# Residual rows loaded late, pair sums over one row, a weight fold moved forward and late loads issued by GpSimd, in a one-core step of a hybrid attention and Fourier network

## The chip, the cores and the metric

The kernel runs on one core of a Trainium2 chip. The metric is the device time of one launch in microseconds (us), taken as the median over several runs. A profile is one execution seen by the hardware profiler. Its engines are PE (TensorE, matmuls; PEld is its weight load), DVE (VectorE), ACT (ScalarE), POOL (GpSimd) and SP (SyncE, which only issues transfers here).

## The reference, cut to what matters

There are 1024 latent tokens and 256 context tokens of width 1024. One even layer and one odd layer run after each other, then a last RMS norm. The shape of the two layers:

```
hl = modulate(rms_norm(xl, norm_g[l]), shift, scale)       # both layers
# even layer: one projection, cut in parts
qa, ka, va, ga, qb, kb, vb, gb = split_even(h @ w_in)
oa = attention over all keys (q and k normed and rotated)  # mixer A, 8 q heads, 2 kv heads
ob = attention over a band of 3 x 128 keys + the context, with a sink logit   # mixer B
y  = concat(oa * silu(ga), ob * silu(gb)) @ w_out
# odd layer
u, gate = split(h @ w_in, 2)
y  = (real(fft2(u)) * silu(gate)) @ w_out
x  = x + gt * y                                            # both layers
```

The keys, the values and the rows after the last norm are the outputs.

## The kernel before, in words

The tokens are cut into ten rows of 128 (tiles 0 to 7 latent, 8 and 9 context). Every matmul is done three times, as hi by hi, hi by lo and lo by hi of operands that `split` (L265 to L283) cuts into a rounded part and a remainder: the hi copy is an ACTIVATE (L277), a DVE copy (L279) or a GpSimd copy, the lo part a subtraction (L283). Which engine takes which is set by letters in tables ("a", "d", "p", or an alternating string such as "pd").

SBUF is cut by hand into zones of equal buffers: 26 in zone u, 8 in w, 4 in p, 3 in pt, 2 in q, 9 short ones in h and 4 short ones in e. `take` hands out a buffer of a zone and `drop` gives it back; whoever takes a buffer next waits for its last reader, including a store to DRAM that reads it. Zone e holds what leaves the attention: the output pieces (`weigh`, L1051 to L1062, two buffers per unit, the second of them stored to `od` in DRAM by SP) and one row of reciprocal sums per tile (`totals`, L1018 to L1032, stored to `scd`).

The profiled execution falls into stages. From 0 to 100 us the conditioning vectors, norms and first projections are made; to about 440 us mixer A is attended; to about 690 us mixer B is attended, with the gate projections (`ga`, stored to `gd` in DRAM) between its units; to 866 us mixer B ends and the even output projection (`oz`) runs; from there come the odd layer's gates (`g1E`, `g1O`, `g1c`), its `u` projection, the Fourier transform and the last projection (`of`).

Attention is done in units: a tile t, a group g (2 and 3 are mixer B) and a pair pr of heads. A unit makes scores (`sC`, L928, against the context; `sB`, L1000, against the band), their maxima (L962, L1006), exponentials (ACT L969), transposes of the probabilities (`pt`, L1045), their hi and lo parts (ACT L277, DVE L1048) and the weighted values (`av`, L1051). Between the units stands filler: a queue of other matmul work, in the order of the string `ORDER`, of which a step runs when the unit's credit (2.9 per unit of mixer B, about microseconds) allows it. The last fillers are: the gates g2 and g3, interleaved by row group; the eight pairs of weight rows of `w_out0` (`wout_next`), loaded by SP into zone h and split into 16 buffers of zone u; the fold f3 of odd weights (`fold_load`, `fold_piece`, tiles `wa30` to `wa33`, L559); and ten steps of the even output projection, one for each row of 128 tokens, in the order of `PAIRS` (0, 4, 2, 6, 3, 7, 1, 5, 8, 9). Such a step may only run when the tiles that it reads are attended, and its load only when seven buffers of zones u and w are free. What is left when the attention ends is drained.

One step of that projection has two parts. `proj_in` (L1210 to L1233) loads a row of attention outputs (`od`, L1215), gates (`gd`, L1218), reciprocal sums (`scd`, L1220, two transfers) and the residual row (`xp`, L1232), multiplies the first three together (L1221, L1222, "pm") and splits the product. `out_proj` (L1235 to L1246) then makes two halves of 24 matmuls each, multiplies by the gate vector (L1243) and adds the residual row (L1244). `proj_step` stores the new row (L1343), takes its squared norm (L1344), and after each second row makes the sum and the difference of the two normed rows (L1356 to L1358), later sums of four rows (L1370 to L1377). These are transposed on PE (`eoE`, `eoO`, `eoC`, L1274) for the odd gates.

The transfers of `proj_in` are issued by GpSimd while the attention runs, and by SP once it has ended (L1211). The order in which each engine finds its instructions is set by a scheduler at build time, which follows the program, the buffers and a model of the times; each engine then works through its own list, and so does each issuing queue.

Of the kernel before, what the change touches and what calls it, by code (L numbers as in the profile page):

```python
# [17 lines left out]
P = 128  # L18
D = 1024
NT = 10  # L20
EPS = 1e-6
GROUPS = ((0, 4, 0), (4, 4, 0), (8, 2, 1))
ZONES = {"u": (26, 1032), "w": (8, 1032), "q": (2, 1024), "pt": (3, 1024), "p": (4, 1280), "h": (9, 512), "e": (4, 256)}
BIG = ("w", "q", "pt", "p", "u")
# [38 lines left out]
E_FQ, E_GD = "d", "d"  # L63
ORDER = "qa0 qa1 kb0 qb0 qb1 g0 g1 g2 g3"
FLATE = "f3"
AT_B = "s"
# [73 lines left out]
def hybrid_step(ctx: ExitStack, tc: tile.TileContext, I, O):  # L140
# [82 lines left out]
    pool.memset(SU, 0.0)  # L223
    rope = cp.tile([P, 8, 96], F32, name="rope")

# [358 lines left out]
    def small_loads(i):  # L584
        if i == 0:
            sp.dma_start(gT, I["gT"])
            sp.dma_start(bT, I["bT"])
            dve.tensor_scalar(bT1, bT[:, :, 8:16], 1.0, None, op0=ALU.add)
        elif i == 1:
            sp.dma_start(rope, I["rope"])  # L590
            sp.dma_start(gk, I["gk"].partition_broadcast(P))
            sp.dma_start(gq, I["gq"].partition_broadcast(P))
        else:
            sp.dma_start(sink, I["sink"].partition_broadcast(P))
            dve.tensor_scalar(nsink, sink, -1.0, None, op0=ALU.mult)
# [104 lines left out]
    def rope_pair(y, n, t, t1, t2):  # L700
        cb = rope[:, t : t + 2, 0:32].unsqueeze(2).to_broadcast([P, 2, 2 * n, 32])
        pick("rope", XE["rope"]).tensor_mul(  # L702
            t1.rearrange("p t h (b c) -> p t (h b) c", b=2), y.rearrange("p t h (b c) -> p t (h b) c", b=2), cb
        )
        for b in range(2):
            o, i = 32 * b, 32 - 32 * b
            sb = rope[:, t : t + 2, 32 + o : 64 + o].unsqueeze(2).to_broadcast([P, 2, n, 32])
            pick("rope", XE["rope"]).tensor_mul(t2[:, :, :, o : o + 32], y[:, :, :, i : i + 32], sb)
        pick("radd", XE["radd"]).tensor_add(t1, t1, t2)
# [389 lines left out]

    def out_weights(src, ks, tags, lc="pd"):  # L1100
        out = []
        for k in ks:
            hi, lo = take(tags, (P, D), F32R), take(tags, (P, D), F32R)
            for hf in range(2):
                raw = take("h", (P, 512))
                sl = slice(hf * 512, hf * 512 + 512)
                sp.dma_start(raw.a, src[k * P : (k + 1) * P, sl])
                split(hi[:, sl], lo[:, sl], raw.a, E_WO, lc)
                drop(raw)
# [25 lines left out]
    def wout_next(n):  # L1135
        for _ in range(n):
            fl_.add(0.0, lambda k=wk_left.popleft(): wout.extend(out_weights(I["w_out0"], (k,), UV)) or 0)

    for i, nm in enumerate(order[:-1]):
# [17 lines left out]
        if i < len(order) - 2:  # L1157
            fl_.add(0.0, releaser(nm))
# [51 lines left out]
    def proj_in(src, gate, r, resid):  # L1210
        ld = sp if gate is None or late[0] else pool  # L1211
        if gate is not None:
# [107 lines left out]
    def proj_step(i, j):  # L1320
# [36 lines left out]
        dve.scalar_tensor_tensor(out=xe.a, in0=xa.a, scalar=rs[:, 0:1], in1=xo_.a, op0=ALU.mult, op1=ALU.add)  # L1357
# [45 lines left out]

    def late_fold(nm):
        def fn():
            ws[nm] = fold_load(int(nm[1]))
            return 0
        return fn

    for n, nm in enumerate(FLATE.split()):  # L1410
        fl_.add(0.0, late_fold(nm))
        if n == 0:
            fl_.add(0.0, lambda: load_to(0), ready=can_run(0, 0))
        for k in range(4):
            fl_.add(FC, lambda k=k, nm=nm: fold_piece(int(nm[1]), k, ws[nm]))
    if not FLATE:
        fl_.add(0.0, lambda: load_to(0), ready=can_run(0, 0))
    for n, ij in enumerate(steps):
# [549 lines left out]
```

## Time and profile before

| What | Value |
|---|---|
| median of 3 runs | 1189.43 us |
| lowest and highest | 1188.47 and 1189.45 us |
| span of the profiled execution | 1196.9 us, 7.5 us above the median |
| PE busy | 1159.1 us, 97% |
| DVE busy | 834.5 us, 70% |
| ACT busy | 577.1 us, 48% |
| POOL busy | 286.0 us, 24% |

No other time of the profiled execution than its span is given, so the span stands for it. A busy time is the time in which an engine worked on at least one instruction. A row of the view by stretches gives the stretch, its length, then busy time (and instructions) of PE, PEld, DVE, ACT and POOL, then the granted TensorE clock (1.00 is full speed), the busy share of the transfer engines and GB/s. A row of the timeline gives start, length, engine, line, operation, tiles, shapes, count, and in brackets the idle time before it with what ended it. In a group of instructions the two numbers behind the bar are busy time in all and mean nanoseconds of one.

### The profile page before, as it was taken

What the parts mean: (1) busy time and instruction counts of PE and PEld (TensorE: products, weight loads), DVE (VectorE), ACT (ScalarE), POOL (GpSimd) and SP (SyncE); (2) the same over time, 40 slices, a digit from 0 to 9 for tenths busy, and PEclk for the clock granted to TensorE, in tenths of its full rate; (3) what the DMA queues carried; (4) which work ended last, traced back from release to release, by engine and by line L of the source; (5) the groups of instructions that cost most, each with busy time, mean ns of one, the idle gap of its engine ahead of it and who ended that gap; (6) DMA issues with size and microseconds to landing.
All of it is one profiled execution on the core that took longest, in us unless ns stands there. A gap on an engine that the chain in (4) does not pass through costs nothing.

```text
span 1196.9 us, 22002 instructions
## 1 busy us (share of the span) xinstructions
PE 1159.1 (97%) x8103; PEld 1037.9 (87%) x8103; DVE 834.5 (70%) x2006; ACT 577.1 (48%) x1159; POOL 286.0 (24%) x272
## 2 busy tenths in 40 slices
PE   8999999999999999999999989998999999999997
PEld 6788899999999998899888878886878888998886
DVE  2489778787777776678888867777755964367543
ACT  4442555555656655556676654532364225333211
POOL 2255644512222230011010035200212226200001
PEclk9999999999999999999999989998998999999999
DMA  9978512323532232444354477774214435364321
GB/s 327 365 257 272 160 59 69 89 77 113 148 89 78 76 95 84 100 120 116 83 148 105 131 223 203 232 224 160 85 45 136 147 115 167 109 186 150 141 105 54
DMA packets 130096, 168.81 MB, mean 141 GB/s; under 512 B 26298, under 2 KB 86454, under 8 KB 129988
## 3 DMA queue, kind: packets, MB, share of 16 engines
q1 hardware_dynamic: 127476, 158.74, 43.5%
q0 software_dynamic: 2368, 8.39, 2.3%
q8 instruction: 64, 1.05, 0.4%
q14 instruction: 44, 0.36, 0.1%
q10 hardware_dynamic: 144, 0.26, 0.1%
HBM read 123.19 MB, written 44.16 MB: 140 GB/s over the span
## 4 chain that ended last, share of the span: by engine, by line
PE 80%; DMA 9%; DVE 5%; ACT 2%; issue 2%; SPq 1%; POOL 1%; POOLq 0%; DVEq 0%; ACTq 0%
PE of L265 9%; PE q L265 8%; PE av L1051 8%; PE pt L1045 8%; PE ga L265 7%; PE sL L928 5%; PE u L265 5%; PE oz L265 4%; PE g1E L265 4%; PE g1O L265 4%; PE kv L265 3%; PE sC L928 2%; PE wa L559 2%; PE g1c L265 2%; DMA h<-i_w_out 2%
## 5 line engine op out<-in xcount | busy, mean ns | idle before, releaser
L277 ACT ACTIVATE pt<-pt 128x512 fp32r<-128x512 f32 (+1 forms) x265 | 146.8, 575 | 107.0 <-PE pt L1045 60.2
L1048 DVE TENSOR_TENSOR pt<-pt,pt 128x512 fp32r<-128x512 f32 (+1 forms) x264 | 170.8, 658 | 37.7 <-ACT pt L277 36.8
L1051 PE MATMUL av<-pt,u 128*128 128x256 f32 x1008 | 167.1, 289 | 0.7 <-ACT pt L277 0.7
L1045 PE MATMUL pt<-identr,p 128*128 128x128 f32 x1008 | 157.4, 273 | 1.1 <-ACT p L969 0.8
L265 PE MATMUL q<-w,u 128*128 128x256 f32 x960 | 143.9, 287 | 0.0
L1051 PEld LDWEIGHTS av<-pt,u 128*128 128x128 f32 x1008 | 138.9, 190 | 4.6 <-ACT pt L277 0.9
L265 PEld LDWEIGHTS q<-w,u 128*128 128x128 f32 x960 | 126.8, 188 | 4.9 <-issue 0.8
L1045 PEld LDWEIGHTS pt<-identr,p 128*128 128x128 f32 x1008 | 119.7, 141 | 8.0 <-ACT p L969 1.0
L969 ACT ACTIVATE p<-p,nm 128x1280 f32<-128x1280 f32 (+1 forms) x80 | 95.5, 1194 | 63.1 <-DVE p L962 62.8
L265 PE MATMUL ga<-u,w 128*128 128x512 f32 (+1 forms) x576 | 124.1, 360 | 0.8 <-DVE byp L1024 0.5
L265 PEld LDWEIGHTS ga<-u,w 128*128 128x128 f32 x576 | 93.6, 188 | 15.2 <-ACT pt L277 1.2
L283 POOL TENSOR_TENSOR w<-h,w 128x512 fp32r<-128x512 f32 x38 | 51.1, 1360 | 143.4 <-DVE w L279 115.0
L928 PE MATMUL sL<-u,q 128*128 128x512 f32 x256 | 82.4, 411 | 2.0 <-DMA q<-qd 2.0
L969 ACT ACTIVATE p<-p,NM 128x640 f32<-128x640 f32 (+2 forms) x80 | 59.2, 740 | 39.5 <-DVE p L962 39.4
L928 PE MATMUL sC<-u,q 128*128 128x256 f32 x320 | 61.8, 294 | 1.6 <-DMA q<-qd 1.0
L962 DVE TENSOR_SCALAR_CACHE_REDUCE p<-sL 128x512 f32<-128x512 f32 x64 | 43.9, 685 | 23.2 <-PE sL L928 14.2
L962 DVE TENSOR_SCALAR_CACHE_REDUCE p<-sL,nm 128x512 f32<-128x512 f32 x64 | 47.7, 745 | 13.7 <-PE sL L928 12.9
L265 PE MATMUL oz<-u,w 128*128 128x512 f32 x192 | 57.3, 403 | 0.0
L283 POOL TENSOR_TENSOR u<-h,u 128x512 fp32r<-128x512 f32 x16 | 20.6, 1293 | 138.0 <-ACT u L277 133.9
L928 PEld LDWEIGHTS sC<-u,q 128*128 128x128 f32 x320 | 48.8, 189 | 5.5 <-issue 1.1
L265 PE MATMUL oz<-u,u 128*128 128x512 f32 x160 | 48.7, 405 | 4.0 <-ACT u L277 2.5
L702 POOL TENSOR_TENSOR h<-h,rope 128x512 f32<-128x512 f32 (+1 forms) x18 | 21.9, 1214 | 126.4 <-ACT h L785 80.5
(728 smaller groups left out, 2569.8 us busy)
## 6 DMA issues: line engine op xcount, KB each, us to landing
q<-qd SPq DMA_DIRECT2D x80, 256.0 KB
h<-i_w_in SPq DMA_DIRECT2D x40, 256.0 KB
p<-i_ada_w SPq DMA_DIRECT2D x18, 512.0 KB
h<-i_w_out SPq DMA_DIRECT2D x32, 256.0 KB
pt<-i_ada_w SPq DMA_DIRECT2D x15, 512.0 KB
qd<-pt SPq DMA_DIRECT2D x20, 256.0 KB
q<-i_ada_w SPq DMA_DIRECT2D x9, 512.0 KB
qd<-q SPq DMA_DIRECT2D x18, 256.0 KB
```

The costliest lines, as they stand in the source:

```text
L265: pe.matmul(out, a, b, start=i == 0, stop=i == n - 1)
L277: act.activation(out, in_, AF.Copy)
L283: pick("lo" + lc, lc).tensor_sub(dst_l, src, dst_h)
L559: pe.matmul(acc[:, i * 256 : i * 256 + 256], wu[j][:, c0 : c0 + P], f[:, j, :], start=j == 0, stop=j == 1)
L702: pick("rope", XE["rope"]).tensor_mul(t1.rearrange("p t h (b c) -> p t (h b) c", b=2), y.rearrange("p t h (b c) -> p t (h b) c", b=2), cb)
L928: pe.matmul(ps, q_at(q, s, hc), keys, start=s == 0, stop=s == 1)
L962: dve.tensor_scalar(p[i][:, end[i] : end[i] + n], ps, sign, last[i], op0=ALU.mult, op1=ALU.min, accum_out=c)
L969: act.activation(p[i][:, 0 : end[i]], p[i][:, 0 : end[i]], AF.Exp, bias=last[i], scale=-1.0, accum_out=SU[:, t, hd + i, 0:1],)
L1045: pe.transpose(tp[:, jj * 256 + i * P : jj * 256 + i * P + P], p[i][:, off : off + P], ident)
L1048: dve.tensor_sub(pt[:, 1, 0:n], tp[:, 0:n], pt[:, 0, 0:n])
L1051: pe.matmul(acc, vv, pt[:, s, jj * 256 : jj * 256 + 256], start=c + jj + s == 0, stop=c + jj == nt - 1 and s == 1,)
```

## The change

It has five parts.

1. The table of cosines and sines (`rope`) is no longer a tile of its own, but three short buffers of zone e, which has seven buffers in place of four. They are loaded by three transfers, and dropped when the projection qb1 has ended; from then on zone e has seven buffers for the attention's outputs.
2. The fold f3 stands in the filler's order between the gates g1 and g2; before, it stood behind all gates and the splits of `w_out0`.
3. For `w_out0` both parts of `split` are GpSimd's: 16 hi copies that were ACT's, and all 16 lo subtractions, of which it had half.
4. The loads of a row of the even projection are issued by GpSimd always, the late ones too, and the residual row is taken and loaded only at the start of `out_proj`.
5. In the pair sums the second normed row is scaled in place, over the row that is being stored to `x1d`, and the difference goes over the first row: two buffers fewer are taken.

```diff
-ZONES = {... "h": (9, 512), "e": (4, 256)}
+ZONES = {... "h": (9, 512), "e": (7, 256)}
-ORDER = "qa0 qa1 kb0 qb0 qb1 g0 g1 g2 g3"
-FLATE = "f3"
+ORDER = "qa0 qa1 kb0 qb0 qb1 g0 g1 f3 g2 g3"
-    rope = cp.tile([P, 8, 96], F32, name="rope")
+    rope = [take("e", (P, 8, 32)) for _ in range(3)]
...
-            sp.dma_start(rope, I["rope"])
+            for i in range(3):
+                sp.dma_start(rope[i].a, I["rope"][:, i])
...
-    def out_weights(src, ks, tags, lc="pd"):
+    def out_weights(src, ks, tags, lc="pd", hc=E_WO):
...
-                split(hi[:, sl], lo[:, sl], raw.a, E_WO, lc)
+                split(hi[:, sl], lo[:, sl], raw.a, hc, lc)
...
+            if nm == "qb1":
+                drop(*rope)
...
-            fl_.add(0.0, lambda k=wk_left.popleft(): wout.extend(out_weights(I["w_out0"], (k,), UV)) or 0)
+            fl_.add(0.0, lambda k=wk_left.popleft(): wout.extend(out_weights(I["w_out0"], (k,), UV, "p", "p")) or 0)
...
+        elif nm[0] == "f":
+            work += [(FC, lambda k=k, nm=nm, j=j: fold_piece(j, k, ws[nm])) for k in range(4)]
...
-        ld = sp if gate is None or late[0] else pool
+        ld = sp if gate is None else pool
...
-        else:
-            for c in range(2):
+            return hi, lo, None
+        for c in range(2):
...
         hi, lo, xr = ins
+        if xr is None:
+            xr = take(OB[0], (P, D))
+            pool.dma_start(xr.a, I["xp"][r * P : (r + 1) * P, :])
...
-        xo_, xe = take(OB[0], (P, D)), take(OB[0], (P, D))
-        act.activation(xo_.a, xb.a, AF.Copy, scale=rs[:, 1:2])
+        xe, xo_ = take(OB[0], (P, D)), xa
+        act.activation(xb.a, xb.a, AF.Copy, scale=rs[:, 1:2])
...
-        drop(xa, xb)
+        drop(xb)
```

What this does to the engines' lists is seen at two places. The first is PE, some 27 us behind the last gate matmul of the profiled execution. Here `wa33` is the last piece of the fold f3, `sC`, `sB`, `pt` and `av` are attention (the digits give tile, group and pair), and `oz00` is the first output projection, of row 0. In the kernel before:

```order
L559 MATMUL wa33_9390<-h923_9286,w924_9288 128x256
L559 MATMUL wa33_9390<-h923_9286,w925_9289 128x256
L928 MATMUL sC9_20_9485<-u438_4475,q944_9420 128x256 x2
L928 MATMUL sC5_30_9692<-u687_7079,q953_9494 128x256 x2
L928 MATMUL sC9_21_9629<-u438_4475,q944_9420 128x256 x2
L1045 MATMUL pt6_310_9639<-identr_85,p948_9444 128x128 x4
L1051 MATMUL av8_21_9465<-pt949_9471,u438_4475 128x256 x4
L265 MATMUL oz00_9552<-u826_8504,w930_9305 128x512
L265 MATMUL oz00_9552<-u827_8505,w930_9305 128x512
```

In the changed kernel `oz00` begins here, three units of attention later:

```order
L1000 MATMUL sB1_310_9936<-u683_7067,q983_9711 128x384 x2
L1045 MATMUL pt5_304_9900<-identr_85,p982_9691 128x128 x2
L1051 MATMUL av9_20_9716<-pt984_9722,u441_4479 128x256 x4
L264 MATMUL oz00_9554<-u850_8685,w943_9398 128x512
L264 MATMUL oz00_9554<-u851_8686,w943_9398 128x512
L1000 MATMUL sB1_311_9941<-u683_7067,q983_9711 128x384 x2
L1045 MATMUL pt5_310_9949<-identr_85,p987_9735 128x128 x4
L928 MATMUL sC1_31_9929<-u685_7069,q983_9711 128x256 x2
L928 MATMUL sC8_30_10062<-u685_7069,q997_9870 128x256 x2
L264 MATMUL oz00_9554<-u850_8685,w944_9399 128x512
```

So `wa30` to `wa33` have gone from this stretch (they stand among the gates now), and between the last gate matmul `ga72` and `oz00` PE finds attention alone: 42 `pt`, 40 `av`, 24 `sC` and 16 `sB` matmuls, with no filler. Behind the last attention unit 237 `oz` matmuls are left, 193 before.

The second place is GpSimd's list at the loads of the first projection rows. `u908` and `u920` are lo parts of `w_out0`; `u927`, `u928` and `u929` are row 0's `od`, `gd` and `scd`, and `w960` belongs to row 4. In the kernel before:

```order
L283 TENSOR_TENSOR u908_9189<-h909_9190,u907_9188 128x512
L1215 DMA u927_9296<-od_72 128x1024
L1232 DMA w932_9309<-i_xp 128x1024
L283 TENSOR_TENSOR u920_9277<-h921_9278,u919_9276 128x512
L1220 DMA u929_9299<-scd_77 64x1024 x2
L1218 DMA u928_9298<-gd_73 128x1024
L1218 DMA w960_9539<-gd_73 128x1024
L1221 TENSOR_TENSOR u928_9298<-u928_9298,u929_9299 128x1024
L1222 TENSOR_TENSOR u927_9296<-u927_9296,u928_9298 128x1024
```

In the changed kernel row 0 has `u940`, `u941` and `u942`, row 4 has `w961`, `w962` and `w963`, and `u935`, `u936` are parts of `w_out0`:

```order
L278 CAST u935_9375<-h937_9377 128x512
L1222 DMA u940_9389<-od_72 128x1024
L1227 DMA w963_9542<-scd_77 64x1024 x2
L282 TENSOR_TENSOR u936_9376<-h937_9377,u935_9375 128x512
L1227 DMA u942_9392<-scd_77 64x1024
L1225 DMA u941_9391<-gd_73 128x1024
L1227 DMA u942_9392<-scd_77 64x1024
L1246 DMA w966_9552<-i_xp 128x1024
L1228 TENSOR_TENSOR w962_9541<-w962_9541,w963_9542 128x1024
L1222 DMA w961_9539<-od_72 128x1024
L1228 TENSOR_TENSOR u941_9391<-u941_9391,u942_9392 128x1024
L1229 TENSOR_TENSOR u940_9389<-u940_9389,u941_9391 128x1024
```

The product of row 0 now stands behind all 16 hi copies of `w_out0`, behind 8 lo subtractions more than before, and behind a product and a load of row 4.

More of the change, by code (lines that the diff above doesn't have):

```diff
@@ L22 @@
 GROUPS = ((0, 4, 0), (4, 4, 0), (8, 2, 1))
-ZONES = {"u": (26, 1032), "w": (8, 1032), "q": (2, 1024), "pt": (3, 1024), "p": (4, 1280), "h": (9, 512), "e": (4, 256)}
+ZONES = {"u": (26, 1032), "w": (8, 1032), "q": (2, 1024), "pt": (3, 1024), "p": (4, 1280), "h": (9, 512), "e": (7, 256)}
 BIG = ("w", "q", "pt", "p", "u")
@@ L700, in rope_pair @@
     def rope_pair(y, n, t, t1, t2):
-        cb = rope[:, t : t + 2, 0:32].unsqueeze(2).to_broadcast([P, 2, 2 * n, 32])
+        cb = rope[0][:, t : t + 2, :].unsqueeze(2).to_broadcast([P, 2, 2 * n, 32])
         pick("rope", XE["rope"]).tensor_mul(
@@ L706, in rope_pair @@
             o, i = 32 * b, 32 - 32 * b
-            sb = rope[:, t : t + 2, 32 + o : 64 + o].unsqueeze(2).to_broadcast([P, 2, n, 32])
+            sb = rope[1 + b][:, t : t + 2, :].unsqueeze(2).to_broadcast([P, 2, n, 32])
             pick("rope", XE["rope"]).tensor_mul(t2[:, :, :, o : o + 32], y[:, :, :, i : i + 32], sb)
@@ L1119, in fn @@
         def fn():
+            if nm[0] == "f":
+                ws[nm] = fold_load(int(nm[1]))
+                return 0
             ws[nm] = load_w(w0cols(base[nm[:-1]] + 256 * int(nm[-1])))
@@ L1156, in hybrid_step @@
             fl_.add(*w)
-        if i < len(order) - 2:
+        if i < len(order) - 2 and nm[0] != "f":
             fl_.add(0.0, releaser(nm))
@@ L1227, in proj_in @@
             drop(ol)
-        else:
-            for c in range(2):
-                split(hi[:, 4 * c : 4 * c + 4, :], lo[:, 4 * c : 4 * c + 4, :], src(c, r), "a", "d")
+            return hi, lo, None
+        for c in range(2):
+            split(hi[:, 4 * c : 4 * c + 4, :], lo[:, 4 * c : 4 * c + 4, :], src(c, r), "a", "d")
         xr = take(OB[0], (P, D))
@@ L1354, in proj_step @@
         kept.clear()
-        xo_, xe = take(OB[0], (P, D)), take(OB[0], (P, D))
-        act.activation(xo_.a, xb.a, AF.Copy, scale=rs[:, 1:2])
-        dve.scalar_tensor_tensor(out=xe.a, in0=xa.a, scalar=rs[:, 0:1], in1=xo_.a, op0=ALU.mult, op1=ALU.add)
-        dve.scalar_tensor_tensor(out=xo_.a, in0=xa.a, scalar=rs[:, 0:1], in1=xo_.a, op0=ALU.mult, op1=ALU.subtract)
-        drop(xa, xb)
+        xe, xo_ = take(OB[0], (P, D)), xa
+        act.activation(xb.a, xb.a, AF.Copy, scale=rs[:, 1:2])
+        dve.scalar_tensor_tensor(out=xe.a, in0=xa.a, scalar=rs[:, 0:1], in1=xb.a, op0=ALU.mult, op1=ALU.add)
+        dve.scalar_tensor_tensor(out=xo_.a, in0=xa.a, scalar=rs[:, 0:1], in1=xb.a, op0=ALU.mult, op1=ALU.subtract)
+        drop(xb)
         if i == 4:
@@ L1401, in load_to @@
         return 0
[L1404 to L1417, printed above, removed]
+    fl_.add(0.0, lambda: load_to(0), ready=can_run(0, 0))
     for n, ij in enumerate(steps):
@@ L1918 @@
     an = np.concatenate([ar, ac], axis=1)
-    rope = np.concatenate([np.cos(an), -np.sin(an), np.sin(an)], axis=1).reshape(8, 128, 96).transpose(1, 0, 2)
+    rope = np.concatenate([np.cos(an), -np.sin(an), np.sin(an)], axis=1).reshape(8, 128, 3, 32).transpose(1, 2, 0, 3)
     i = np.arange(128)
```

## The prediction

> **What bounds the kernel now.** I read the page first, then the busy time by stretches, then the timeline of PE where it falls short, then the waits and the chain for the causes.
>
> ```profile
> PE 1159.1 (97%) x8103; PEld 1037.9 (87%) x8103; DVE 834.5 (70%) x2006; ACT 577.1 (48%) x1159; POOL 286.0 (24%) x272
> 600.00:690.00 90.00, 87.55 (x592) 79.31 (x591) 76.68 (x236) 61.05 (x142) 9.84 (x8) 1.00 0.48 126
> 690.00:820.00 130.00, 117.28 (x636) 99.98 (x635) 93.16 (x212) 59.62 (x136) 33.03 (x32) 0.96 0.73 218
> 820.00:866.00 46.00, 46.00 (x197) 37.20 (x197) 34.06 (x46) 17.28 (x27) 9.10 (x8) 0.96 0.33 115
> ```
>
> PE is the bound, and no matmul is taken out. A change can only win what PE idles, or what it runs at less than full clock. Nearly all that the change touches lies between 600 and 866 us, where PE idles 90.00 - 87.55 = 2.45 us and 130.00 - 117.28 = 12.72 us. From 820 to 866 it is full.
>
> The second loss is the clock. Five microseconds at a time:
>
> ```profile
> 695.00:700.00 5.00, 1.73 (x4) 1.49 (x5) 2.31 (x7) 3.20 (x7) 2.54 (x4) 0.74 0.54 187
> 700.00:705.00 5.00, 5.00 (x22) 4.44 (x22) 2.65 (x8) 2.33 (x7) 0.83 (x2) 0.57 0.95 275
> 815.00:820.00 5.00, 1.77 (x6) 1.34 (x7) 3.47 (x4) 2.37 (x4) 0.31 (x1) 0.69 0.89 256
> 820.00:825.00 5.00, 5.00 (x15) 3.92 (x15) 4.00 (x6) 2.02 (x2) 0.00 (x0) 0.63 0.49 159
> 100.00:105.00 5.00, 2.66 (x80) 2.10 (x68) 4.97 (x12) 0.84 (x3) 2.15 (x3) 1.00 0.72 238
> ```
>
> Work at clock 0.57 takes 1/0.57 of its time, so of 5.00 us of busy time 2.15 are lost, and 1.73 x 0.26 = 0.45 before that: 2.6 us. At 815 to 825 it is 0.55 + 1.85 = 2.4 us. Both follow an idle stretch of 4 us or more. The last row is the other case: PE is idle for 47% of it, in 80 short matmuls' gaps, and the clock stays at 1.00.
>
> So the stage loses 2.45 + 12.72 + 2.6 + 2.4 = **20.2 us**. The four largest pieces of idle time on PE, and behind them what stood on the chain or kept ACT:
>
> ```profile
> 698.27 3.75 PE L559 MATMUL wa<-h,w 128*128 128x256 f32 x8 [4.51 <-ACT pt L277]
> 736.84 3.48 PE L265 MATMUL oz<-u,u 128*128 128x512 f32 x14 [1.59 <-DVE h L1243]
> 815.78 0.55 PE L1274 MATMUL eoE<-identr,p 128*128 128x128 f32 x3 [1.96 <-DVE p L1370]
> 818.78 1.22 PE L265 MATMUL oz<-u,u 128*128 128x512 f32 x2 [2.45 <-ACT u L277]
> 719.70 9.74 DMA od<-e
> 803.27 6.01 DMA u<-gd
> ACT u L277 <- DMA h<-i_w_out: 6.6, 1, 6.6
> ACT e L1030 <- DMA od<-e: 9.5, 1, 9.5
> ```
>
> The first gap names ACT's `pt`, but ACT itself had stood 6.6 us at the hi copy of a `w_out0` row that had not landed, with the attention's copies queued behind it. The other three belong to zone e: DVE or ACT wants a buffer that a store to `od` still reads, and what stands behind it on that engine (products, the squared norm, the hi copy `u`) comes late.
>
> **Part 1, zone e.** With seven buffers three more stores may be under way before `take` waits. A unit of attention holds one until its store has ended, and five units end in the 24 us of the stretch below, so three buffers cover some 15 us. The longest wait, 9.74 us, is shorter. I let these waits go: 1.59 + 1.96 + 2.45 us and the 2.4 us of clock. What is late next is in part 4. The three loads of the table lie at the start, and I take them at 0 (between -0.5 and +1 us).
>
> **Part 3, the splits of `w_out0`.** ACT is freed of 16 copies, and so of the wait: 4.51 us of idle time and 2.6 us of clock go. The cost falls on GpSimd.
>
> ```profile
> 681.19 2.99 PE L265 MATMUL ga<-u,w 128*128 128x256 f32 x24
> 687.39 2.70 PE L265 MATMUL ga<-u,w 128*128 128x256 f32 x21 [0.47 <-DVE byp L1024]
> L283 POOL TENSOR_TENSOR u<-h,u 128x512 fp32r<-128x512 f32 x8 | 10.3, 1293 | 111.9 <-ACT u L277 107.7 <-PE sB L1000 4.2
> L279 DVE CAST w<-h 128x512 fp32r<-128x512 f32 x36 | 16.7, 492 | 10.7 <-DMA h<-i_w_in 9.4 <-PE q L265 1.0 <-PE ga L265 0.3
> L1222 POOL TENSOR_TENSOR w<-w,w 128x1024 f32<-128x1024 f32 x3 | 7.8, 2613 | 0.3 <-DMA w<-od 0.2
> L1220 POOL DMA_DIRECT2D w<-scd x4 | 2.2, 547 | 0.8 <-issue 0.5 <-POOL w L1222 0.3
> w<-gd POOLq DMA_DIRECT2D x3, 512.0 KB, 7.6
> POOL w L1215 <- DMA od<-e: 6.2, 1, 6.2
> ```
>
> No GpSimd copy of 128x512 is in the trace. Its ends are DVE's copy, 0.49 us, and GpSimd's own subtraction, 1.29; I take 0.8, nearer to DVE's, which reads one operand too. In GpSimd's new list 8 copies, 8 subtractions and 10 transfers stand between the release by the gate `ga71` and the load of row 0's `od`: 8 x 0.8 + 8 x 1.29 + 10 x 0.55 = 22.2 us (19.7 to 26.1). From `ga71` to the last gate `ga72` lie four gates, 6.2 us apart as above: 24.8 us. So GpSimd is level with PE when `ga72` ends (call it T0) and can load row 0's `od`, for which it waits on `ga72`. Then come six more issues and a split, 0.55 x 6 + 1.29 = 4.6 us, the landing of `gd`, 7.6, and the two products of row 0, 2 x 2.6, which is some 17 us behind T0. A load of row 4 between them waits for a store to `od`, as now for 6.2 us, which `gd`'s landing hides.
>
> **Part 2, the fold.** The four `wa` pieces move from this stretch to one in which PE is full; they cost there what they save here. But they were filler. Between `ga72` and `oz00` PE now has attention alone:
>
> ```profile
> 723.80 1.43 PE L1051 MATMUL av<-pt,u 128*128 128x256 f32 x10
> 725.06 0.60 PE L1045 MATMUL pt<-identr,p 128*128 128x128 f32 x4
> 725.42 0.48 PE L928 MATMUL sC<-u,q 128*128 128x256 f32 x2
> 725.74 0.86 PE L1000 MATMUL sB<-u,q 128*128 128x384 f32 x4
> 726.44 5.71 PE L265 MATMUL oz<-u,w 128*128 128x512 f32 x24
> L1048 DVE TENSOR_TENSOR pt<-pt,pt 128x512 fp32r<-128x512 f32 x25 | 16.7, 677 | 0.2 <-ACT pt L277 0.2
> L962 DVE TENSOR_SCALAR_CACHE_REDUCE p<-sC,nsink 128x256 f32<-128x256 f32 x25 | 11.5, 469 | 0.8 <-PE sC L928 0.6
> L962 DVE TENSOR_SCALAR_CACHE_REDUCE p<-p,nm 128x384 f32<-128x384 f32 x12 | 7.0, 599 | 0.0
> L1006 DVE SCALAR_TENSOR_TENSOR p<-sB,maskf 128x384 f32<-128x384 f32 x12 | 6.4, 544 | 2.3 <-PE sB L1000 2.3
> L1062 DVE TENSOR_TENSOR e<-av,e 64x256 f32<-64x256 f32 x16 | 6.6, 410 | 5.3 <-DMA od<-e 3.2 <-ACT e L1060 2.1
> L283 DVE TENSOR_TENSOR u<-u,w 128x1024 fp32r<-128x1024 f32 x2 | 2.4, 1213 | 0.0
> L1021 DVE TENSOR_SCALAR tot<-tot 128x16 f32<-128x16 f32 x5 | 0.8, 161 | 0.0
> ```
>
> By the distances from start to start, 40 `av` at 0.126, 42 `pt` at 0.09, 24 `sC` at 0.16 and 16 `sB` at 0.175 make 5.0 + 3.8 + 3.8 + 2.8 = 15.4 us. DVE's list in the same piece of the program has 10 of L1048, 11 and 6 of L962, 8 of L1006, 5 of L1062, six small ones like L1021, and row 0's lo part, without which `oz00` can't go on: 6.8 + 5.2 + 3.6 + 4.4 + 2.1 + 1.0 + 1.2 = 24.3 us. GpSimd's product at 17 us, with its hi and lo part behind it (some 2.4, by DVE's 1.2 each), is there at 19.4 and hidden. So DVE sets the end, and PE idles **8.9 us** in short pieces, as at 100 to 105 us, where the clock stayed.
>
> One page's rule speaks against such pieces. The Trainium skill, TensorE: Matmul & The Clock Gate, section A second HAM failure mode: psum-queue depth-cycling, says that frequent micro-idles between groups of matmuls make the clock fall and rise again. The row at 100 to 105 us disagrees. It is the fourth rival below.
>
> **Part 4, the late loads.** Before, SP issued them; now they stand in GpSimd's list at 0.55 us each, behind products of 2.6 us and behind each other's waits. At the end DVE waits for the last loads (rows 1 and 5), and its lo parts behind them wait too. PE has 237 `oz` matmuls left there, but in their order the third matmuls of `oz50` and `oz11` need those lo parts. The price is between 0 (several rows of 24 matmuls, 5.7 us each, cover it) and 6.0, the longest wait for `gd` on the chain at the same place now. I take what DVE does after such a load, two products and a lo part: 3 x 1.22 = **3.7 us**. The late residual row costs nothing: it is needed only behind 24 matmuls of 5.7 us, about what a transfer of its size takes.
>
> Here another rule would give less. The Trainium skill, DMA: Bandwidth & Descriptors, section Issuing engines are not separate DMA queues, says that all transfers share the same 16 engines and that another issuer saves only the time of issuing, small beside the transfer. By that this part would cost nothing, and the sum would be 3.7 us lower. The 7.6 us of landing against 0.55 us of issue agree; what waits in GpSimd's list ahead of an issue is not in the rule.
>
> **Part 5, the pair sums.** ACT scales a row in place and so waits for its store to `x1d`; behind it on ACT stand the next row's norm and, in the drain, hi copies. PE is full there (46.00 of 46.00 us from 820 to 866), so between 0 and +1 I put 0.
>
> **The sum.** Lost after: 1.0 of the 2.45 us ahead of 690 (its waits, too, were mixed with the hi copies of `w_out0`), 8.9 in the filler-less stretch, 3.7 at the last rows, 1.0 of small waits as now: 14.6 us. Gain 20.2 - 14.6 = 5.6 us. From the span of 1196.9 that is 1191.3; the runs lie 7.5 us under the span, so their median comes to **1183.8 us**.
>
> **The rivals.**
>
> *More is kept.* A DVE instruction starts before the one ahead of it has ended:
>
> ```profile
> 810.58 0.69 DVE L1244 TENSOR_TENSOR pt<-pt,h 128x512 f32<-128x512 f32 x1
> 811.19 1.28 DVE L1357 SCALAR_TENSOR_TENSOR pt<-w,r11y,p 128x1024 f32<-128x1024 f32 x1
> ```
>
> That is 0.08 us; if all 47 of the stretch do so, they give back 3.7 us, and the last loads may be covered. Then 1.0 + 5.2 + 0 + 1.0 = 7.2 us are lost: gain 13.0, 1176.4 us. PE's longer backlog speaks for it, the one queue of GpSimd against it.
>
> *The stores weren't late for want of buffers.* If `od` stores and row loads are late because of the queues, seven buffers move the wait from zone e to the row products, and the 8.4 us at 735 and 812 to 825 stay beside 3.7 less: 14.6 + 8.4 - 3.7 = 19.3 lost, 1188.5 us, no difference. For it: the chain carries loads of rows too (6.01 us `u<-gd`), not `od` alone.
>
> *A store holds up GpSimd (slower).* Row 0's products stand behind row 4's load, which waits for tile 7's store to `od`. Stores of that kind held POOL for 6.2 us, and once for longer:
>
> ```profile
> POOL e L1512 <- DMA od<-e: 19.0, 1, 19.0
> ```
>
> If GpSimd stands 19.0 us from some 5 us behind T0, row 0's products are done at 29, its hi and lo part at 31.4, 7.1 us behind DVE's 24.3. The units are used up by then, so this is one piece, with 2.6 us of clock behind it, and part 4 goes to its 6.0: 12.0 us more, 1195.8 us. It decides from a wait of about 12 us on. A copy of 1.8 us or more would do the same, for which no row speaks.
>
> *The clock falls in the filler-less stretch (slower).* At half clock its 15.4 us of matmuls take 30.8, which is 6.5 above DVE's 24.3, and 2.6 us follow: 1192.9 us. It decides once PE's share of busy time there, 15.4 of 24.3 or 63%, is too low to hold the clock. Against it: at 100 to 105 us 53% held it.
>
> **How the numbers follow.** A measurement of this kernel can tell about 0.2%, 2.4 us, from no change: faster is below 1187.05, slower above 1191.8. The forecast gets 0.45, more kept 0.16, no difference 0.22, the store 0.08, the clock 0.09. Of the forecast's spread (part 4's 0 to 6.0, the table, part 5, 1183.8 -4.2 to +4.3) about a tenth falls within 0.2%; of the no difference a fifth is faster, and of the clock's case two fifths, milder, within. Faster: 0.40 + 0.16 + 0.04 = 0.60; within: 0.05 + 0.14 + 0.04 = 0.23; slower: 0.04 + 0.08 + 0.05 = 0.17. The range from 1177.0 to 1192.5 leaves out the lower half of the first rival, the store's case and the clock's upper half.
>
> **What would show it.** Right: ACT's wait for `i_w_out` and the waits for `od<-e` gone; PE below 70% busy at clock 1.00 for some 24 us behind `ga72`, released by DVE; an idle piece of 2 to 6 us at `oz50` or `oz11`. Wrong: a gap of over 4 us ahead of `oz00` ended by row 0's products on POOL (the store's case), clock rows of 0.5 to 0.7 in that stretch (the clock's), waits for `od<-e` as long as now (no difference), and a median above 1187.

## The result, and the profile after

The changed kernel took 1208.47 us in the median of 4 runs (1204.61 to 1211.85), the kernel before 1189.44 us: a ratio of **1.0146 (95% interval 1.0119 to 1.0174)**, 1.5% slower, where 1183.8 us had been forecast. One profiled execution is behind each page, and executions of one kernel differ by several microseconds: the changed kernel's took 1207.86 us at a span of 1206.1.

The page's first row, and the busy time by stretches:

```profile
PE 1157.3 (96%) x8103; PEld 1033.3 (86%) x8103; DVE 831.4 (69%) x1994; ACT 572.5 (47%) x1147; POOL 323.4 (27%) x326
600.00:690.00 90.00, 88.94 (x582) 80.52 (x581) 73.53 (x234) 55.60 (x130) 20.50 (x22) 1.00 0.42 108
690.00:820.00 130.00, 112.32 (x649) 96.32 (x650) 93.24 (x214) 57.26 (x133) 52.37 (x62) 0.95 0.67 191
820.00:866.00 46.00, 44.54 (x192) 34.94 (x191) 32.25 (x40) 14.18 (x19) 13.72 (x16) 1.00 0.53 175
```

The rows by stretches have the columns that were explained above. The same matmuls take the same busy time. PE idles 17.68 us from 690 to 820 us, 12.72 in the first profile of the kernel before. Most of that is one place, in rows of five microseconds and on PE's timeline:

```profile
710.00:715.00 5.00, 3.00 (x20) 2.11 (x19) 4.34 (x16) 4.31 (x15) 4.43 (x7) 1.00 0.99 237
715.00:720.00 5.00, 0.00 (x0) 0.00 (x0) 0.00 (x0) 0.00 (x0) 0.00 (x0) 0.57 1.09 250
720.00:725.00 5.00, 0.00 (x0) 0.00 (x0) 0.00 (x0) 0.00 (x0) 2.33 (x1) 0.50 1.05 225
725.00:730.00 5.00, 3.50 (x17) 3.53 (x18) 2.14 (x6) 0.51 (x2) 0.87 (x2) 0.57 0.85 186
```

```profile
713.05 0.66 PE L1045 MATMUL pt<-identr,p 128*128 128x128 f32 x4
726.50 0.76 PE L928 MATMUL sC<-u,q 128*128 128x256 f32 x2 [12.79 <-DMA q<-qd]
742.34 5.37 PE L264 MATMUL oz<-u,w 128*128 128x512 f32 x22 [0.63 <-DVE w L282]
```

For ten microseconds no engine computes, but for one product on GpSimd, and the transfer engines are full (the last column but one, 1.09 and 1.05). PE waits 12.79 us for a q load, in the stretch without filler behind the last gate. What the transfer engines carry is seen on the issuers. SP issues the second half of that load at 712.68, GpSimd two rows' loads around it:

```profile
709.93 0.59 SPq L933 DMA_DIRECT2D q<-qd  x1
712.68 0.63 SPq L933 DMA_DIRECT2D q<-qd  x1
```

```profile
690.55 0.61 POOL L278 CAST u<-h 128x512 fp32r<-128x512 f32 x1 [8.50 <-DMA h<-i_w_out]
707.46 0.61 POOL L278 CAST u<-h 128x512 fp32r<-128x512 f32 x1 [6.31 <-DMA h<-i_w_out]
708.01 0.58 POOL L1222 DMA_DIRECT2D u<-od  x1
710.47 1.04 POOL L1227 DMA_DIRECT2D w<-scd  x2 [1.88 <-DMA scd<-e]
713.30 0.55 POOL L1225 DMA_DIRECT2D u<-gd  x1
714.36 0.57 POOL L1246 DMA_DIRECT2D w<-i_xp  x1
720.06 2.33 POOL L1228 TENSOR_TENSOR w<-w,w 128x1024 f32<-128x1024 f32 x1 [5.14 <-DMA w<-scd]
729.11 0.61 POOL L1222 DMA_DIRECT2D w<-od  x1 [6.72 <-DMA od<-e]
732.22 2.39 POOL L1229 TENSOR_TENSOR u<-u,u 128x1024 f32<-128x1024 f32 x1
```

256 KB issued at 712.68 are used at 726.50, 13.8 us later. Between 708 and 715 GpSimd let go 2.5 MB (one `od`, two pairs of `scd`, one `gd`, one residual row). The last number of each row below is the time from issue to landing. The `od` row, the first of them, needed 4.0 us; the other 2 MB needed 8.6 to 14.0 us:

```profile
u<-od POOLq DMA_DIRECT2D x1, 512.0 KB, 4.0
w<-scd POOLq DMA_DIRECT2D x2, 256.0 KB, 8.6
u<-scd POOLq DMA_DIRECT2D x2, 256.0 KB, 10.0
u<-gd POOLq DMA_DIRECT2D x1, 512.0 KB, 10.6
w<-i_xp POOLq DMA_DIRECT2D x1, 512.0 KB, 14.0
```

Of the forecast's signs, the first came: on DVE and ACT no wait for `od<-e` is left, and ACT's wait for `i_w_out` is gone from this stage and stands on GpSimd instead, where a copy takes 616 ns (the rows below). The others did not: behind `ga72` the longest piece ends with a transfer and not with DVE, the clock falls, and at the last projection rows PE's longest idle piece is 1.11 us.

```profile
POOL u L278 <- DMA h<-i_w_out: 16.6, 4, 8.5
L278 POOL CAST u<-h 128x512 fp32r<-128x512 f32 x16 | 9.8, 616 | 87.8 <-DMA h<-i_w_out 46.4 <-PE ga L264 41.4
```

### The profile page after: what moved, and what is told of

Read it like the earlier page. It is cut to its first block, busy times and chain, and to the rows that moved or that the text cites. A ratio compares the mean times of both kernels' runs of the same rounds, so it can differ in the third digit from the quotient of the medians.

```text
span 1206.1 us, 22001 instructions
## 1 busy us (share of the span) xinstructions
PE 1157.3 (96%) x8103; PEld 1033.3 (86%) x8103; DVE 831.4 (69%) x1994; ACT 572.5 (47%) x1147; POOL 323.4 (27%) x326
## 3 DMA queue, kind: packets, MB, share of 16 engines
q8 instruction: 64, 1.05, 0.4%
## 5 line engine op out<-in xcount | busy, mean ns | idle before, releaser
L264 PEld LDWEIGHTS ga<-u,w 128*128 128x128 f32 x576 | 93.8, 188 | 17.2 <-ACT e L1060 2.5
L264 PE MATMUL oz<-u,w 128*128 128x512 f32 x304 | 83.0, 397 | 1.4 <-DVE w L282 1.0
L264 PEld LDWEIGHTS oz<-u,w 128*128 128x128 f32 x304 | 56.2, 188 | 14.8 <-DVE w L282 1.7
L962 DVE TENSOR_SCALAR_CACHE_REDUCE p<-sL,nm 128x512 f32<-128x512 f32 x64 | 47.7, 746 | 13.9 <-PE sL L928 13.2
L702 POOL TENSOR_TENSOR h<-h,e 128x512 f32<-128x512 f32 (+1 forms) x18 | 21.9, 1219 | 125.8 <-ACT h L785 79.9
L264 PE MATMUL of<-u,u 128*128 128x512 f32 (+1 forms) x174 | 55.4, 386 | 0.0
```

What stands on the lines that cost most here:

```text
L264: pe.matmul(out, a, b, start=i == 0, stop=i == n - 1)
L702: pick("rope", XE["rope"]).tensor_mul(t1.rearrange("p t h (b c) -> p t (h b) c", b=2), y.rearrange("p t h (b c) -> p t (h b) c", b=2), cb)
L962: dve.tensor_scalar(p[i][:, end[i] : end[i] + n], ps, sign, last[i], op0=ALU.mult, op1=ALU.min, accum_out=c)
```

## The experiments

All ratios are against the kernel before, run beside them on the same chip, with their 95% intervals; two versions are called different only where their intervals lie apart. "Lost" below is PE's idle time and busy x (1 - clock), added over rows of two microseconds of the profiled execution. That is one execution; the last column says how far its run lay above (+) or below the median of its kernel. For the first profile of the kernel before, whose run has no time of its own, this is an estimate: its span of 1196.9 us and the 1.8 us by which the changed kernel's span lies below its run. The names: zone e (part 1), fold (part 2), splits (part 3), late loads and residual row (the two halves of part 4), pair sums (part 5).

| Kernel | ratio (interval) | lost 690 to 760 | lost 760 to 870 | run against median |
|---|---|---|---|---|
| before, first profile | | 10.1 | 8.2 | about +9 |
| before, second profile | 0.9996 (0.9969 to 1.0023) | 2.6 | 6.7 | -1.2 |
| changed | 1.0146 (1.0119 to 1.0174) | 17.6 | 2.9 | -0.6 |
| changed, splits undone | 1.0243 (1.0208 to 1.0278) | 7.9 | 21.9 | -0.7 |
| changed, fold undone | 1.0142 (1.0100 to 1.0184) | 8.1 | 14.5 | -1.4 |
| changed, late loads undone | 1.0137 (1.0099 to 1.0174) | 21.2 | 5.4 | +1.0 |
| changed, residual row undone | 1.0100 (1.0054 to 1.0147) | 15.2 | 5.8 | -1.0 |
| changed, pair sums undone | 1.0086 (1.0055 to 1.0118) | 15.1 | 0.0 | -3.7 |
| changed, zone e undone | 1.0158 (1.0112 to 1.0203) | 17.2 | 11.5 | +1.3 |
| before + zone e | 1.0060 (1.0031 to 1.0090) | 6.1 | 12.3 | +3.0 |
| before + fold | 1.0079 (1.0053 to 1.0104) | 13.2 | 4.3 | +3.0 |
| before + splits | 1.0007 (0.9991 to 1.0024) | 9.0 | 8.5 | +4.1 |
| before + residual row | 1.0065 (1.0042 to 1.0089) | 3.5 | 12.7 | -2.5 |
| before + pair sums | 1.0052 (1.0034 to 1.0070) | 7.0 | 12.1 | +6.4 |
| changed, fold and pair sums undone | 1.0059 (1.0040 to 1.0078) | 8.4 | 9.8 | -0.1 |
| changed, less to load | 1.0186 (1.0152 to 1.0221) | 14.8 | 12.3 | -2.4 |
| changed, q earlier | 1.0115 (1.0086 to 1.0145) | 17.5 | 6.0 | -0.4 |
| changed, q earlier, pair sums undone | 1.0125 (1.0101 to 1.0150) | 14.5 | 9.3 | +0.6 |

**The kernel before, again.** No edit.

> The kernel before, unchanged, for a second profile of it. Its profiled execution of before had a span of 1196.9 us, 7.5 us above the median; the changed kernel's span is 1.8 us below its own run. If spans always lie 1.8 us below the run, the execution shown in the first profile was itself some 9 us slower than usual, and this one should have a span of about 1187.6 us. Then one of the two large pieces that the prediction counted, 4.51 + 2.6 us at 698 or 1.96 + 2.45 + 2.4 us at 816, should be missing or much shorter. If the 7.5 us are the profiler's, the span is again near 1197.

The span was 1189.6 us. The 6.6 us that ACT had stood for `i_w_out` are 1.4 here and the piece at 698 is gone; the piece at 816 is there, 1.17 + 2.45 us:

```profile
690.00:820.00 130.00, 122.32 (x676) 104.69 (x675) 100.90 (x221) 64.08 (x143) 33.36 (x32) 0.99 0.75 225
707.65 0.48 PE L928 MATMUL sC<-u,q 128*128 128x256 f32 x2 [1.64 <-DMA q<-qd]
809.06 0.55 PE L1274 MATMUL eoE<-identr,p 128*128 128x128 f32 x3 [1.17 <-DVE p L1370]
812.06 0.73 PE L265 MATMUL oz<-u,u 128*128 128x512 f32 x2 [2.45 <-ACT u L277]
ACT u L277 <- DMA h<-i_w_out: 1.4, 1, 1.4
```

So the execution on which the prediction rested had a stall that this one does not have, and the runs side with this one. PE idles 7.68 us in this stretch, not 12.72, at a clock of 0.99. This is the profile with which the others are compared.

**The splits undone.**

```diff
-            ... out_weights(I["w_out0"], (k,), UV, "p", "p")) or 0)
+            ... out_weights(I["w_out0"], (k,), UV)) or 0)
```

> The changed kernel with the splits of w_out0 as before (hi copies on ACT, lo parts on GpSimd and DVE in turn). Theory of the bundle: GpSimd's list with 16 more copies runs late, then lets go 2.5 MB of row loads within 7 us, and the attention's q load, issued among them, needs 13.8 us: PE idles 12.8 us. Without the copies the loads go earlier and apart: gap below 6 us, 1195 to 1200 us. Theory of the filler: the gap is there because the fold is gone from it, whoever splits w_out0: 1204 to 1210 us.

Neither theory's time came. The loss behind the last gate fell from 17.6 to 7.9 us as the first theory wanted (the wait for q is 3.33 us), and the kernel got slower by 1%: 21.9 us are lost at the end of the attention, the largest piece this one:

```profile
828.13 1.22 PE L264 MATMUL oz<-u,w 128*128 128x512 f32 x2 [5.33 <-DVE e L1062]
```

**The fold undone.** The fold stands behind the gates again (`FLATE = "f3"`, `ORDER` without f3).

> The changed kernel with the fold f3 late again, behind the gates. Theory of the filler: its 7.6 us of matmuls lie under the wait for q and the gap falls by about that: 1198 to 1201 us. Theory of the bundle: the row loads stay bunched; f3's own matmuls stand in PE's list ahead of the wait or behind it, and only what stands ahead helps: 1202 to 1209 us.

The filler does lie under the wait: 8.1 us lost in place of 17.6. But what is saved there is lost again where the last rows are projected:

```profile
710.72 1.19 PE L929 MATMUL sC<-u,q 128*128 128x256 f32 x4 [3.69 <-DMA q<-qd]
813.23 1.22 PE L1052 MATMUL av<-pt,u 128*128 128x256 f32 x4 [4.09 <-DVE e L1063]
819.95 7.13 PE L265 MATMUL oz<-u,w 128*128 128x512 f32 x24 [5.50 <-DVE e L1063]
```

**The late loads undone.** `ld = sp if gate is None or late[0] else pool`.

> The changed kernel with the late loads, those after the attention, issued by SP again. The bundle lies before the attention's end and stays: 1204 to 1209 us by both theories. If the late loads on GpSimd were the cause (the prediction's part 4, 3.7 us), 1203 to 1205 us, and PE's short idle pieces between 785 and 830 us go.

No difference can be told from the changed kernel, and the wait for q is there again, 12.88 us. The late loads on GpSimd are not the cause.

**The residual row undone** (taken and loaded in `proj_in`).

> The changed kernel with the residual row taken and loaded in proj_in again, one buffer more for each waiting row. Theory of the bundle, in its later form: what the versions with +1.4% share is that fewer buffers and GpSimd's list let two rows' loads go together with the q loads. With the residual row back in proj_in, the condition of seven free buffers is met later and the rows come apart: 1193 to 1200 us, and the wait for q under 6 us. Theory of the filler (the fold's place alone): no difference to the changed kernel, 1205 to 1211 us.

1.0100, below the changed kernel's 1.0146, but the intervals overlap, and the time lies between the two theories'. The wait for q is 6.55 us.

**The pair sums undone** (rows of their own).

> The changed kernel with the pair sums over rows of their own, as before. The in-place scaling waits for the store to x1d (5.6 us once on ACT in the profile of the changed kernel); the pair sums lie behind the wait for q. Theory of the bundle: 1204 to 1209 us, the wait for q stays at 12 us or so. If the in-place pair sums are the cause, PE's idle pieces at 785 to 830 and 880 to 890 us go, some 4 us: 1201 to 1205 us.

About 0.6% better. The wait for q stays, 10.49 us. From 760 to 870 us 0.0 us are lost in place of 2.9, but this execution is 3.7 us faster than the kernel's median, so the usual run may lose more.

**Zone e undone** (four buffers, the table a tile of its own).

> The changed kernel with the table of cosines as a tile of its own and four buffers in zone e. By the prediction's part 1 the waits for od stores come back: 6 to 8 us more, 1212 to 1217 us. By the loss of 3 us in the first 100 us of the changed kernel (11.36 idle against 8.39), which would be the three loads' doing: 3 us less at the start. If zone e was never the bound: 1203 to 1208 us.

No difference to the changed kernel (1.0158 and 1.0146, with intervals that overlap). The wait for q is not there; in its place DVE waits for zone e, and PE for DVE:

```profile
725.83 2.47 PE L1050 MATMUL av<-pt,u 128*128 128x256 f32 x10 [9.66 <-DVE e L1061]
```

Seven buffers take this wait away, and the q load is late instead, in the same crowd of transfers.

**Zone e alone.**

```diff
-"e": (4, 256)}
+"e": (7, 256)}
-    rope = cp.tile([P, 8, 96], F32, name="rope")
+    rope = [take("e", (P, 8, 32)) for _ in range(3)]
...
```

> The kernel before with only the table moved and seven buffers in zone e. By the prediction's part 1 the waits for od stores go, which in the second profile of before are 1.17 + 2.45 us at 809 to 814 us: 3 to 5 us faster than before. If those waits only move, within 2 us of before. If the three loads cost 3 us at the start, 0 to 3 us slower.

Slower by 0.6%, which none of the three expectations had. Waits for `od<-e` are all but gone on ACT (0.3 us), and at the longest piece DVE now stands for a row of reciprocal sums that hasn't landed, with the attention's `e` and the copy `ssp` behind it:

```profile
821.53 1.22 PE L1052 MATMUL av<-pt,u 128*128 128x256 f32 x4 [6.14 <-DVE ssp L1354]
819.92 1.23 DVE L1224 TENSOR_TENSOR q<-q,u 128x1024 f32<-128x1024 f32 x1 [2.88 <-DMA u<-scd]
```

**Less to load.** For rows 0 and 4, GpSimd writes constants over the buffers of the reciprocal sums and the residual row, which aren't loaded; the two rows' results are not those of the reference.

```diff
+            if r in (0, 4):
+                pool.memset(rl.a, 1.0)
+            else:
...
+            if r in (0, 4):
+                pool.memset(xr.a, 0.0)
+            else:
```

> The changed kernel, in which rows 0 and 4 of the even projection load no reciprocal sums and no residual row: GpSimd writes ones and zeros into these buffers in their place (about 0.95 us each, as it takes to issue the two transfers). 1.5 to 2 MB go out of the crowd of transfers at 707 to 727 us, in which the q load needed 13.8 us at about 0.23 MB per us. Theory that the transfer engines are full there: the wait for q falls by 6 to 9 us, from 12.8 to under 6, and the time by as much with the clock's share: ratio to before about 1.005 to 1.008 in place of 1.015. Theory that GpSimd's list or the missing filler sets the end: the gap only changes its name, ratio 1.012 to 1.016.

The wait for q fell by 5.4 us to 7.39, somewhat less than the first theory has it; this fits that these rows held up the q load. Yet the kernel got no faster: 1.0186, above both theories' ranges, with an interval that overlaps the changed kernel's. The loss is at the last rows, where it had been small:

```profile
719.61 0.77 PE L928 MATMUL sC<-u,q 128*128 128x256 f32 x2 [7.39 <-DMA q<-qd]
826.49 2.08 PE L264 MATMUL oz<-u,p 128*128 128x512 f32 x4 [4.51 <-ACT p L276]
831.56 2.08 PE L264 MATMUL oz<-u,u 128*128 128x512 f32 x4 [3.00 <-ACT u L276]
```

**The fold alone.**

```diff
-ORDER = "qa0 qa1 kb0 qb0 qb1 g0 g1 g2 g3"
-FLATE = "f3"
+ORDER = "qa0 qa1 kb0 qb0 qb1 g0 g1 f3 g2 g3"
...
```

> The kernel before with only the fold moved between the gates. If the filler is what hides the transfers: PE stands for q or for row 0 behind the last gate, 5 to 10 us: ratio 1.004 to 1.009. By the prediction's own sum for this part, 8.9 us: 1.0075. If the fold's place doesn't matter: within 0.998 to 1.002.

1.0079, 9.4 us, in the first theory's range and near the prediction's 8.9 us. 13.2 us are lost behind the gates in place of 2.6. PE's longest wait there ends with a transfer, and the clock is 0.56 from 720 to 730 us:

```profile
719.93 1.19 PE L927 MATMUL sC<-u,q 128*128 128x256 f32 x4 [3.09 <-DMA od<-e]
```

**The splits alone** (`"p", "p"` in `wout_next`).

> The kernel before with only the splits of w_out0 given to GpSimd. By the prediction's part 3, ACT's wait goes (it was 1.4 us, not 6.6, in the second profile of before): ratio 0.998 to 1.000. If GpSimd's list holds up the row loads, which then go out together: the waits for q and for rows grow, ratio 1.004 to 1.01.

No difference: what ACT is freed of was worth nothing in usual executions, and GpSimd carries the copies. (The 17.5 us lost in the profile are those of an execution 4.1 us above the median.)

**The residual row alone.**

```diff
         hi, lo, xr = ins
+        if xr is None:
+            xr = take(OB[0], (P, D))
+            pool.dma_start(xr.a, I["xp"][r * P : (r + 1) * P, :])
...
```

> The kernel before with only the residual row's load moved to the start of out_proj, issued by GpSimd. By the prediction: costs nothing, ratio 0.998 to 1.002. From the changed kernel, which is 0.4% better without this part: ratio 1.003 to 1.006, with PE or DVE waiting for i_xp or for what stands behind it in GpSimd's list.

0.65% slower. DVE stands 11.1 us for the gates of a last row, which SP had issued at 809.78 and DVE could use at 820.85; ACT's hi part waits behind it, and PE for that. DVE's wait for a residual row itself is 0.3 us.

```profile
DVE pt L1221 <- DMA pt<-gd: 11.1, 1, 11.1
824.48 1.22 PE L265 MATMUL oz<-u,u 128*128 128x512 f32 x2 [7.83 <-ACT u L277]
```

**Two q loads earlier.** The loads for tiles 5 and 1 are taken one tile earlier, in a buffer of zones u or w.

```diff
+            if pr == QPRE and (t, g) in Q_AT:
+                n2 = next((u[:2] for u in units[n:] if u[:2] not in ((t, g), nx)), None)
+                if n2 is not None and n2 not in qs:
+                    qs[n2] = load_q(*n2, zs=("u", "w"))
...
```

> The changed kernel with two of the late q loads (tiles 5 and 1 of group 3) taken one tile earlier, into a buffer of zones u or w, so that they are issued ahead of the crowd of row loads. If the q load is what PE lacks behind the last gate: the wait of 12.8 us falls under 4 us, and the loss of 17.6 us between 690 and 760 us to 9 or less (DVE's list, as in the prediction): ratio 1.006 to 1.009. If the same crowd only makes something else late (row 0's product, a store of zone e), the loss stays over 13 us: ratio 1.012 to 1.016.

The wait for q is gone, and the loss is what it was, 17.5 us: PE now waits for ACT, which waits to write a row of reciprocal sums ("issue": the profile names nothing that released it); the clock falls to 0.50.

```profile
728.91 1.97 PE L1046 MATMUL pt<-identr,p 128*128 128x128 f32 x8 [6.48 <-ACT e L1031]
ACT e L1031 <- issue: 6.8, 1, 6.8
```

The ratio, 1.0115, lies between the two theories' ranges; the loss speaks for the second.

**The same, pair sums undone.**

> The same early q loads, with the pair sums over rows of their own as before. Undoing the pair sums alone gave 1.0086. If q and the pair sums are two separate causes: 1.000 to 1.003. If the crowd makes something else late: 1.006 to 1.009.

In neither range (1.0125): with the early q loads no difference that the pair sums make can be told. The two are not separate causes whose prices add.

**The pair sums alone.**

```diff
-        xo_, xe = take(OB[0], (P, D)), take(OB[0], (P, D))
-        act.activation(xo_.a, xb.a, AF.Copy, scale=rs[:, 1:2])
+        xe, xo_ = take(OB[0], (P, D)), xa
+        act.activation(xb.a, xb.a, AF.Copy, scale=rs[:, 1:2])
```

> The kernel before with only the pair sums done in place. From undoing them in the changed kernel (1.0146 to 1.0086): ratio 1.004 to 1.007, with ACT waiting for the store to x1d, and DVE behind it, between 760 and 870 us. By the prediction's part 5 (0 to +1 us): 0.999 to 1.001.

0.5% slower, as expected from undoing them, but not by the expected wait: ACT stands for the store to `x1d` for 1.4 us only. In the profiled execution, which is 6.4 us above the median, the longest piece is again at the last rows, where DVE stands for a row of reciprocal sums:

```profile
820.06 7.45 PE L265 MATMUL oz<-u,w 128*128 128x512 f32 x24 [5.55 <-DVE e L1062]
818.39 1.23 DVE L1221 TENSOR_TENSOR u<-u,w 128x1024 f32<-128x1024 f32 x1 [4.21 <-DMA w<-scd]
```

**Fold and pair sums undone together.**

> The changed kernel without the moved fold and without the in-place pair sums: zone e, the splits of w_out0, GpSimd's late loads and the late residual row remain. If filler and pair sums are all that costs: 0.997 to 1.002, with less than 9 us lost between 690 and 760 us and less than 6 between 760 and 870. If the remaining parts cost on their own, as the singles for zone e (1.006) and the residual row (1.0065) say: 1.006 to 1.012.

1.0059, at the lower edge of the second expectation: the remaining parts are not harmless. Behind the gates 8.4 us are lost, as expected of the fold; from 760 to 870 it is 9.8, not under 6.

No version was faster than the kernel before.

## Why the prediction was wrong, point by point

In the prediction's own terms, 20.2 us were to be lost from 600 to 866 us before the change and 14.6 after it. Measured to 870 us, it is 12.5 us in the second profile of the kernel before and 21.6 in the changed kernel. Both ends of the subtraction failed. No rival had the time either; the slowest of them was put at 1195.8 us.

**The base, "so the stage loses 20.2 us", failed.** 4.51 + 2.6 us of it were a stall of one execution. The sign was in the table: the span stood 7.5 us above the median. The prediction took that for an offset between span and runs; the changed kernel's span lies 1.8 us below its own run, and the second span of before is 7.3 us lower with the stall gone. A term of 7.1 us that the usual run doesn't lose can't be won, and moving the splits alone won nothing (1.0007). In the company of the other parts the moved splits do help: undoing them there costs 1%.

**Part 1 failed: "I let these waits go".** They went, and nothing was won. With seven buffers the loss in the two stretches is 20.5 us, with four 28.7, in one execution each, at ratios that can't be told apart; alone, the edit costs 0.6%. This is nearest to the second rival, that the stores weren't late for want of buffers and the wait moves to the rows' products. It had 0.22 and the price of no difference. The next thing late was named in part 4 only, with 3.7 us; it was a q load, a row of reciprocal sums or a `gd` row, by the kernel.

**Part 3 was right in its sizes.** GpSimd's copy takes 0.616 us (0.8 taken, 0.49 to 1.29 allowed), and GpSimd loads row 0's `od` at 708.01, 1.9 us behind the start of the last gate matmul at 706.1, which the prediction called level. From there on it was wrong: row 0's second product ended at 734.6, some 28 us behind T0, where 17 had been forecast, since the loads took 8.6 to 14.0 us in place of 7.6 and the wait for `od<-e` (6.72 us) was not hidden. PE, late by its wait for q already, then waited 0.63 us for row 0's lo part.

**Part 2 failed in "so DVE sets the end".** A transfer set it: PE stood 12.79 us for a q load, 17.6 us were lost there in place of 8.9, and DVE itself waited 12.4 us for PE. The sum counted the engines' lists in this stretch and no transfer, though PE had waited 0.96 us for a q load at 716.64 in the first profile, and a row quoted in the prediction (700 to 705 us) has the transfer engines at 0.95. In the kernel before the same crowd is there (the transfer engines' share is 0.98 from 692.3 to 713.1 us in the second profile) and PE has the fold to do. That the fold alone costs 9.4 us, near the 8.9 of the sum, is luck: its longest wait behind the gates ended with a transfer, and part of the loss is elsewhere; of the 17.5 us lost from 690 to 870 us there 7.4 are the clock's, of which the sum had nothing. "They cost there what they save here" failed by a little: in all ten kernels that have the fold between the gates, 1.2 to 3.8 us are lost from 440 to 600 us (in the changed kernel a gate waits 1.87 us for ACT at 556.66, ahead of the fold), and nothing in the eight profiles that have it late.

**Part 4's price was right by chance, its edit was not free.** 2.9 us are lost from 760 to 870, 3.7 forecast, but in pieces of 1.11 us at most and not in one of 2 to 6 us at `oz50` or `oz11`; SP's issuing in place of GpSimd's changes nothing that can be told (1.0137). The Trainium skill's rule (DMA: Bandwidth & Descriptors, Issuing engines are not separate DMA queues) was weighed there for the issuer alone, and the trace agrees with it. Its first half, that all transfers share the same engines, should have been weighed in part 2: 256 KB took 13.8 us among 2 MB of rows. "The late residual row costs nothing" failed: 0.65% alone, though no engine was seen to stand long for that row itself.

**Part 5 failed: "I put 0".** In place, the pair sums cost 0.52% alone and about 0.6% in the change, where ACT once stood 5.6 us for the store to `x1d`:

```profile
ACT w L1366 <- DMA x1d<-w: 5.6, 1, 5.6
```

Alone that wait was 1.4 us, so it is not shown that this is what the price consists of.

**The clock rival's low rows came, but not by its mechanism.** Behind the gap PE worked in pieces at full clock:

```profile
735.00:740.00 5.00, 4.34 (x25) 3.15 (x25) 5.00 (x16) 4.83 (x13) 3.08 (x3) 1.00 0.84 231
740.00:745.00 5.00, 4.37 (x22) 3.36 (x21) 5.00 (x15) 3.31 (x7) 1.04 (x2) 1.00 0.79 202
```

From 690 to 820 us the clock was 0.50 to 0.57 only in and behind the ten idle microseconds. The stretch with PE busy for 63% did not come about, so at that share the rival is not tested; in the rows above it is 87%. The Trainium skill's rule on micro-idles (TensorE: Matmul & The Clock Gate, A second HAM failure mode: psum-queue depth-cycling) finds no case in these rows. The prediction saw low rows behind idle stretches of 4 us or more; in the 18 profiles of this case shorter ones were enough, as said at the end. The store's rival had the place right (a wait for `od<-e` in GpSimd's list ahead of row 0's products, 6.72 us) and not the size.

**What stays open.** Single parts cost 0.79, 0.65, 0.60, 0.52 and 0.07%, 2.6% in all, and the whole 1.46% (the late loads were not run alone). What is shown: when the q load's wait was taken away or made shorter (fold undone, splits undone, zone e undone, q earlier, less to load), the loss came back between 690 and 870 us, with another wait at the same place (zone e, q) or at the last projection rows (fold, splits, transfers). What is shown of these rows is that the engines stand in order behind a row that hasn't landed: ahead of the late pieces DVE waited for a row of reciprocal sums with the splits undone (4.66 us), the fold undone (3.20), zone e alone (2.88) and the pair sums alone (4.21), and for a `gd` row with the residual row alone (11.06). The prediction had these sums (`scd`) only as issues in GpSimd's list. Why each of zone e, residual row and pair sums alone brings these rows late is not settled: each edit also made the scheduler write a new order on all engines, and no run kept the order and changed the buffer alone.

Some of the loss also lies outside the stage that the prediction and these runs looked at. Counted as in the table but over the whole span, 53.3 us are lost in the changed kernel and 37.7 in the second profile of before; these 15.6 us are nearly all of the 16.5 between the spans, and 11.2 of them lie between 690 and 870 us. Of the rest 3.1 lie in the first 100 us. The three loads of the table are not shown to be the reason: with zone e undone 10.3 us are lost there, and with the pair sums alone, which also has one load, 12.6, against 11.4 in the changed kernel.

## What to carry to other kernels

Before a stall is counted as winnable, hold the profiled span against the median of the runs; if it stands well above, some of its idle time is not in the usual run. The same holds for each profile taken later. When filler is moved away from a place, count the transfers that it covers there, not the engines' lists alone: here the crowd of transfers made one load or another late in version after version. And in a stage with several in-order lists, an edit that takes one wait away is worth what the next late thing leaves, which a run of that edit alone tells sooner than a sum.

## What was not expected of the hardware

A 256 KB load needed 13.8 us when 2 MB of others were issued between 710 and 715 us, around it. Loads of the same kinds of rows landed in 4.7 to 7.3 us between 690 and 720 us of the first profile, with one at 10.2, and in 8.6 to 14.0 us here. GpSimd copies 128x512 elements in 616 ns, under half of the 1.29 us of its two-operand subtraction. Between 690 and 870 us of the 18 profiles PE stood still 40 times for 2 us or more. At the end of all but two of these pieces (2.52 us each, with the residual row alone) a row of two microseconds shows a clock below 0.6; so it does for 8 of the 27 pieces of 0.9 to 1.5 us, some of which lie close behind longer ones. The kernel before itself ran between 1185.5 and 1198.3 us in 13 runs on another chip, much wider than the 1188.47 to 1189.45 us of the first three runs.
